# A hybrid DeltaNet and attention block: low parts of the projection weights moved to VectorE, the triangular substitution moved to GpSimd

## The chip, the cores and the metric

The kernel runs on one core of a Trainium2 chip. The metric is the device time of one execution in microseconds, the median of several runs. Engines are named as in the profile: PE is TensorE (PEld its weight loads), DVE is VectorE, ACT is ScalarE, POOL is GpSimd, SP is the engine that issues the transfers.

## The reference, cut to what matters

One layer over 512 latent and 256 context tokens of width 2048. All projections read the same normalised, modulated input `h`. Eight heads run a gated delta rule in chunks of 64 tokens, once in each direction; eight heads run attention with rotary positions; one output projection follows.

```python
qkv_g, z_g, gates, q_a, k_a, v_a, z_a = split_proj(h @ w_in)        # and the same for the context
qkv = silu(centred_conv(qkv_g, conv_w))                             # 5 taps, depthwise
...
# chunk_gated_delta, per head and direction
diff = g_c[..., :, None] - g_c[..., None, :]
decay = where(incl, exp(where(incl, diff, 0.0)), 0.0)
a = where(strict, einsum('nbhid,nbhjd->nbhij', k_beta, k_c) * decay, 0.0)
t_inv = triangular_solve(eye + a, eye, left_side=True, lower=True)  # 64 x 64 per chunk
u = t_inv @ (v_c * b_c)
w = t_inv @ (k_beta * exp(g_c))
def step(s, inp):                                                   # over the chunks, in order
    v_new = u_i - w_i @ s
    o_i = (q_i * exp(g_i)) @ s + intra_i @ v_new
    s = s * exp(g_last) + (k_i * exp(g_last - g_i)).T @ v_new
...
o_gdn = o_lf + flip(o_lb)                                           # the two directions
gdn = rms_norm(o_gdn, gdn_norm_w) * silu(z_g)
y = concatenate([gdn, attention(...) * silu(z_a)]) @ w_out
```

## The kernel before, in words

**Numbers in two parts.** Every large matmul is done in three passes of a fast 32-bit format. A weight piece of 128 x 512 is loaded (`wraw`), ACT casts it to the high part (`whi`), and the difference `wraw - whi` is the low part (`wlo`, line 130, helper `split`). PE multiplies high by high, high by low and low by high. `wraw`, `whi` and `wlo` have three buffers each. The engine that makes the low part is POOL unless the call names another. `proj_steps` makes one projection tile of 128 columns out of four such pieces (line 159); there are 36 of these tiles (k, q, v of the scan heads, k and v of attention, q of attention, and five tiles of attention's gate z), the rest of z is projected later by `z_piece`, and the output weights by the last stage.

**Order of work.** PE's instructions run in program order up to the output projection. For the other engines and for SP's transfers a scheduler lays down each queue's order when the kernel is built, by priority (program order, lowered by a stated offset for `first_of_all`, 2500, and `soon` or the substitution, 1500) and by its own model of the times. On the chip each queue is in order.

**Stages.** (1) Normalisation and the first head's projections, to about 160 us. (2) Eight scans, one head after the other, about 243 to 905 us. (3) Attention with the remaining z projections. (4) Output projection.

**A scan** (`gdn_scan(h)`) has 12 chunk steps, both directions stacked on the partitions. For each step PE multiplies keys and state (`ks`, lines 852 to 857), DVE forms `r` (line 866, two halves), PE applies the triangular inverse `UU` (`ts`, line 875), ACT scales to `vs` and `vn` (879, 882), PE updates (886), and DVE adds the new state `st` (892) to `sd`, the decayed old state, which POOL has made meanwhile (called through `mul`, line 240). Between these, the scan yields three times per step and `pull(n)` puts some `n` columns of projection matmuls for later heads into PE's order (3900, 2700 and 3200 columns). These yields are counted as slots, 35 in a scan.

**Preparing the next head** (`gdn_prep(h + 1)`) is cut into eleven parts which are put in at the slots of `PREP_AT`. In order: transposes of k and their norms (three parts; the third also forms `gr`, the decay, from a broadcast load minus `gcum`, line 681, cut by masks at 684 and raised by ACT); products with decay (the fourth); and in the fifth the matrix `AT`, its transposed blocks `NT`, and the **substitution**: 96 blocks of 16 x 16 (`NE`) are read back through DRAM, and 14 pairs of small operations on `NE` invert them:

```python
for m in range(14, 0, -1):
    n = 15 - m
    ... tv = NE[:, 0:m, m] x NE[:, m, m+1:]      # m x n products per partition
    ... NE[:, 0:m, m+1:] += tv
```

The result goes to DRAM (`nd2`, line 744). Parts six and seven transpose v (`tv`, line 751, two banks of PSUM shared with other small tiles) and scale it into `vtok` on ACT; after the seventh the blocks come back as `DD` (four loads, line 758) and are transposed to `DT` (763). Parts eight to eleven (slots 27 to 33) join the blocks on PE (`pxa` 771, `pxb` 779, `pxy` 801 to 813) into `UU`, with copies by ACT (790), POOL (792) and DVE (821).

During a scan, DVE also does the convolution and SiLU of the heads projected meanwhile (`conv`, lines 217 to 225; `silu`, 237; v's result is `vv`). At a scan's end POOL adds the decayed outputs (`oq`, line 902) before DVE and ACT normalise them. In the last scan there is no next head; `attn_prep` normalises and rotates attention's k and the first q instead (`rope_apply`, product `t2` on POOL, the rest on DVE).

The first head is prepared ahead of the first scan, its parts put in by a list of pulls; two gate steps (`g1`) and head 1's convolutions stand among them.

Of the kernel before, what the change touches and what calls it, by code (L numbers as in the profile page):

```python
# [11 lines left out]
ALU = mybir.AluOpType  # L12
# [56 lines left out]
def build(tc, a):  # L69
    nc = tc.nc  # L70
    V, S, G, T, SY = nc.vector, nc.scalar, nc.gpsimd, nc.tensor, nc.sync
# [31 lines left out]
    def hpass(k, hi, lo):  # L103

        return (hi, [t[:, k] for t in hh]), (hi, [hl(m, k) for m in range(2)]), (lo, [t[:, k] for t in hh])
# [13 lines left out]
    gsc = {}  # L119
# [6 lines left out]
    def split(raw, nm, lo_eng=None):  # L126
        hi = wp.tile([128, 512], F32R, tag="whi", bufs=3, name=f"whi_{nm}")
        lo = wp.tile([128, 512], F32R, tag="wlo", bufs=3, name=f"wlo_{nm}")
        S.copy(hi, raw)  # L129
        (lo_eng or G).tensor_tensor(out=lo, in0=raw, in1=hi, op=ALU.subtract)  # L130
        return hi, lo

    def wpiece(src, nm, shape, lo_eng=None):
        raw = wp.tile([128, 512], F32, tag="wraw", bufs=3, name=f"wraw_{nm}")
        v = raw
        if shape is not None:
            v = raw.rearrange("p (a b) -> p a b", b=shape)
        SY.dma_start(v, src)
        hi, lo = split(raw, nm, lo_eng)
        if shape is not None:  # L140
            hi = hi.rearrange("p (a b) -> p a b", b=shape)
            lo = lo.rearrange("p (a b) -> p a b", b=shape)
        return hi, lo
# [6 lines left out]
    def proj_tile(col, nm, pl, pc=None):  # L150
        for _ in proj_steps(col, nm, pl, pc):
            pass

    def proj_steps(col, nm, pl, pc=None):


        for kq in range(4):
            src = w_in[kq * 512:(kq + 1) * 512, col:col + 128].rearrange("(k p) c -> p k c", p=128)
            hi, lo = wpiece(src, f"{nm}_{kq}", 128)
            passes = [(kq * 4 + k4, n, lw, rt) for k4 in range(4)  # L160
                      for n, (lw, rt) in enumerate(hpass(kq * 4 + k4, hi[:, k4], lo[:, k4]))]

            def one(out, m, k, n, lw, rt):
                T.matmul(out, lhsT=lw, rhs=rt[m], start=k == 0 and n == 0, stop=k == KT - 1 and n == 2,  # L164
                         skip_group_check=True)

            if pc is not None and kq == 0:
                for out, m, n_ in ((pl, 0, SEQ), (pc, 1, CTX)):
                    for x in passes:
                        one(out, m, *x)  # L170
                        yield n_
                continue
            for x in passes:
                one(pl, 0, *x)
                if pc is not None:
                    one(pc, 1, *x)
                yield SEQ if pc is None else SEQ + CTX
# [11 lines left out]
    def btile(shape, nm):  # L189
        return PB.tile(shape, F32, tag="b", name=nm)  # L190
# [45 lines left out]
    def silu(eng, out, x, t):  # L236
        eng.scalar_tensor_tensor(out=out, in0=t, scalar=1.0, in1=x, op0=ALU.add, op1=ALU.mult)

    def mul(eng, out, x, y):
        eng.tensor_tensor(out=out, in0=x, in1=y, op=ALU.mult)  # L240
# [347 lines left out]
    def kq_of(h):  # L588
        if h not in kqs:
            kqs[h] = qkp.tile([128, 8, 128], F32, tag="kq", bufs=3, name=f"kq{h}")  # L590
        return kqs[h]

    def gdn_post_k(h, raw):
        kq = kq_of(h)
        kc = kcs[h] = qkp.tile([128, 2, 2, 64], F32, tag="kc", bufs=2, name=f"kc{h}")
        acc, e, off = conv(8 + h, f"k{h}", raw, True)
        x, y = [t[:, off:off + SEQ].rearrange("p (c t) -> p c t", t=64) for t in (acc, e)]
        silu(V, kq[:, 0:4, 0:64], x[:, 0:4], y[:, 0:4])
        silu(V, kq[:, 4:8, 64:128], x[:, 4:8], y[:, 4:8])
        x, y = [t[:, 0:CTX].rearrange("p (c t) -> p c t", t=64) for t in (acc, e)]  # L600
        silu(V, kc[:, :, 0], x[:, 0:2], y[:, 0:2])
        silu(V, kc[:, :, 1], x[:, 2:4][:, ::-1], y[:, 2:4][:, ::-1])
# [18 lines left out]
    def gdn_prep(h):  # L621


        nm = f"h{h}"
        kq, kc, vv = kqs[h], kcs[h], vvs[h]
        UU, IB = UUs[h % 2], IBs[h % 2]
        col = slice(h * 12, h * 12 + 12)
        gr = gp.tile([128, 12, 64], F32, tag="gr", bufs=1, name=f"gr{nm}")
        for s in range(2):
            src = growd[s:s + 1, col].rearrange("s r t -> s (r t)").to_broadcast([64, 768])  # L630
# [7 lines left out]
        t2 = btile([128, 4, 128], f"t2{nm}")  # L638
# [17 lines left out]
        for p in range(2):  # L656
# [18 lines left out]
                        in0=gsc["beta"][:, col].rearrange("p (v q) -> p v q", v=2),  # L675
                        in1=rk2.unsqueeze(1).to_broadcast([128, 2, 6]), op=ALU.mult)
# [1 line left out]
        mul(V, cc[:, 2], cc[:, 0], gsc["esuf"][:, col])  # L678


        G.tensor_tensor(out=gr, in0=gr, in1=gsc["gcum"][:, col].unsqueeze(2).to_broadcast([128, 12, 64]),
                        op=ALU.subtract)
        for v in range(2):
            V.tensor_tensor(out=gr[:, v * 6:v * 6 + 6], in0=gr[:, v * 6:v * 6 + 6],
                            in1=masks[v].unsqueeze(1).to_broadcast([128, 6, 64]), op=ALU.min)
# [35 lines left out]
        NE = gp.tile([96, 16, 16], F32, tag="NE", bufs=1, name=f"NE{nm}")  # L721
        for half in range(2):
            for blk in range(2):
                b, bi = half * 64 + blk * 32, half * 2 + blk
                cb = slice(blk * 32, blk * 32 + 32)
                for v in range(2):
                    src = AT[b:b + 32, v * 6:v * 6 + 6, cb] if v == half else NT[b:b + 32, :, cb]
# [6 lines left out]
        with tc.high_priority(offset=1500):  # L734
            for m in range(14, 0, -1):
                n = 15 - m
                tv = tm[:, :m * n].rearrange("w (j i) -> w j i", i=n)
                V.tensor_tensor(out=tv, in0=NE[:, 0:m, m:m + 1].to_broadcast([96, m, n]),
                                in1=NE[:, m:m + 1, m + 1:].to_broadcast([96, m, n]), op=ALU.mult)
                V.tensor_tensor(out=NE[:, 0:m, m + 1:], in0=NE[:, 0:m, m + 1:], in1=tv, op=ALU.add)  # L740
        nd2 = nd2s[h % 2]
        for s in range(2):
            ds_ = slice(16 * s, 16 * s + 16)
# [40 lines left out]
        for bi in range(4):  # L784
            half, b = bi // 2, bi * 32
            for v in range(2):
                src = (DD if v == half else DT)[b:b + 32, v * 6:v * 6 + 6]
# [36 lines left out]
    def gdn_scan(h):  # L824

        nm = f"h{h}"
        kq, kc = kqs[h], kcs[h]
# [4 lines left out]
        oq = gp2.tile([128, 2, 4, 128], F32, tag="oq", bufs=1, name=f"oq{nm}")  # L832
        osb = oq[:, 0]
        kss = stile([128, 2, 256], f"ks{nm}", "k")
        steps = [(0, 0), (0, 1), (1, 1), (1, 0)] + [(0, p) for p in range(2, 6)] + [(1, p) for p in range(5, 1, -1)]
        for si, (v, p) in enumerate(steps):
# [8 lines left out]
            if si == 0:  # L845
                r = vtok[:, p]
            else:
                ks = kss[:, si % 2].rearrange("q (d e) -> q d e", d=2)
                r = gp2.tile([128, 128], F32, tag="r", bufs=1, name=f"r{nm}_{si}")
# [9 lines left out]
                with first_of_all():  # L859
# [5 lines left out]
                    for rows, d in halves:  # L865
                        V.scalar_tensor_tensor(out=r[rows], in0=ks[rows, d], scalar=gsc["negeg"][rows, gcol:gcol + 1],  # L866
                                               in1=vtok[rows, p], op0=ALU.mult, op1=ALU.add)
# [31 lines left out]
        ms = gp2.tile([128, 4], F32, tag="ms", bufs=2, name=f"ms{nm}")  # L899
        oc = gp2.tile([128, 8, 64], F32, tag="oc", bufs=1, name=f"oc{nm}")  # L900
        jk = oc[:, 0:2].rearrange("p c t -> p (c t)")
        G.tensor_tensor(out=oq[:, 1], in0=osb, in1=oq[:, 1], op=ALU.add)
        V.tensor_tensor(out=osb, in0=oq[:, 1], in1=o, op=ALU.add)
        for p in range(4):
            S.activation(jk, osb[:, p], AF.Square, accum_out=ms[:, p:p + 1])
# [15 lines left out]
    def swapped(x):  # L921

        return x.rearrange("p t (a s r) -> p (t a) s r", a=2, s=2)[:, :, ::-1]
# [17 lines left out]

    def rope_apply(y, tb, t2):

        mul(G, t2.rearrange("p t (a s r) -> p (t a) s r", a=2, s=2), swapped(y),
            tb[:, 1].rearrange("p t (a s r) -> p (t a) s r", a=2, s=2))
        mul(V, y, y, tb[:, 0])
        V.tensor_tensor(out=y, in0=y, in1=t2, op=ALU.add)
# [76 lines left out]
        split_from(tp.rearrange("p t c -> p (t c)"), *A["qt"])  # L1024

    F1, F2, F3 = 3900, 2700, 3200
    PREP_AT = (0, 2, 4, 6, 8, 10, 12, 27, 29, 31, 33)

    def soon():
        return tc.high_priority(offset=1500)  # L1030
# [4 lines left out]
    with tc.high_priority(offset=4000):  # L1035
        raws = [take(klat, cctx[:, 0]), take(qlat, None), take(vlat, cctx[:, 1], None, V),
                take(klat1, cctx1[:, 0], xraw[0]), take(qlat1, None, xraw[1])]
# [82 lines left out]
    def pull(n):  # L1120
        debt[0] += n
        while debt[0] > 0:
            c = next(feed, None)
            if c is None:
                debt[0] = 0
                return
            debt[0] -= c

    def run(gen, *pulls):

        for n in pulls:
            pull(n)
            if next(gen, gen) is gen:
                return
        for _ in gen:
            pull(2000)

    g0, g1 = gates(0, 1), gates(1, NH)
# [7 lines left out]
    with first_of_all():  # L1146
        next(g0, None)
    prep = gdn_prep(0)
    for i, n in enumerate((3000, 5500, 5500, 4000, 14000, 6000)):
        pull(n)  # L1150
        next(prep, None)
        if i == 4:
            gdn_post_k(1, raws[3])
    pull(3000)
    next(g1)
    pull(9000)
    with first_of_all():
        next(g1)
    gdn_post_q(1, raws[4])
    es_x.close()  # L1160
    run(g1, 14000)
    es1.close()
    gp2 = es_g.enter_context(tc.tile_pool(name="gp2", bufs=1, reuse_waits="tile"))
    UUs.append(gp2.tile([128, 12, 128], F32, name="UU1"))
# [3 lines left out]
    for h in range(NH):  # L1168
# [3 lines left out]
        if h + 1 < NH:  # L1172
            prep, prep_at = gdn_prep(h + 1), PREP_AT
        else:
# [4 lines left out]
            prep, prep_at = attn_prep(), range(1, 36, 2)  # L1179
# [334 lines left out]
    for c in range(4):  # L1514
# [3 lines left out]
        if c < 3:  # L1518
            ops = [PO.tile([128, 512], F32, tag="po", name=f"po{c}_{t}") for t in range(4)]
            for k in range(KT):  # L1520
                hi, lo = wpiece(w_out[k * 128:(k + 1) * 128, cs_], f"wo{c}_{k}", None, V)
# [6 lines left out]
        for k in range(KT):  # L1528
            hi = op_.tile([128, 512], F32R, name=f"wlh{k}")
            lo = op_.tile([128, 512], F32R, name=f"wll{k}")  # L1530
# [5 lines left out]
        for t in range(4):  # L1536
# [5 lines left out]
            f = fr[:, t:t + 1]  # L1542
# [36 lines left out]
```

## Time and profile before

| | |
|---|---|
| median of 3 runs | 1368.79 us (1368.75 to 1371.78) |
| profiled execution | 1373.23 us, of which the span from first to last instruction is 1371.5 |
| mean granted clock of TensorE | 0.979 |
| busy: PE / DVE / ACT / POOL | 1271.3 / 781.6 / 583.7 / 458.2 us |
| the same from 243 to 905 us (the scans) | 611.7 / 382.2 / 309.0 / 270.1 us of 662 |

How to read the rows: a row of a group or of a line gives the source line, the engine, the operation, output and inputs by the program's names, their shapes, and the count. Where three durations stand, they are the shortest, median and longest in ns, followed by when the first and the last one started. A row in order of time begins with the start and the duration in us; "x3" are three instructions in a row, and a bracket gives the engine's idle time before it and what ended that. A row of the list of waits says who waited for whose result: us in total, times, longest. A row by stretch gives the stretch, its length, the busy time and count of each engine, then the clock and the transfers' share and rate.

### The profile page before, as it was taken

To read this page: it belongs to the slowest core of one execution; us is meant where nothing else is said; L and a number is where in the kernel's file an instruction comes from. 1 tells how busy PE (TensorE), PEld (TensorE's weight loads), DVE (VectorE), ACT (ScalarE), POOL (GpSimd) and SP (SyncE) were. 2 spreads that over 40 slices of the span, in tenths; PEclk is the share of its full clock that TensorE was granted. 3 is DMA by queue.
4 is the path that set the end of the run, shared out by engine and by line. 5 is a ranking of instruction groups with operands and counts; after the bars stand their busy time and mean duration, and the time that the engine had idled before them with its cause. 6 is when DMAs were issued, how large, how long until landed. Compare 5 with 4: busy or idle time off the path is not lost. (4 is left out here: it accounts for less than half of the span.)

```text
span 1371.5 us, 24428 instructions
## 1 busy us (share of the span) xinstructions
PE 1271.3 (93%) x9226; PEld 1032.2 (75%) x9226; DVE 781.6 (57%) x1662; ACT 583.7 (43%) x1464; POOL 458.2 (33%) x437
## 2 busy tenths in 40 slices
PE   6899998999899999999899998998999999999997
PEld 4566777877788778877787777777888788777785
DVE  5455594766846666485664524316788877544322
ACT  4222542535345454544545434434455444433211
POOL 1323232434344253434334344443233232020330
PEclk9999999999999999999999999999999999999998
DMA  9999233221332223231222443347344343564212
GB/s 342 323 334 348 56 94 85 60 63 44 71 75 70 50 66 65 71 72 53 51 59 70 98 128 100 89 135 226 108 124 146 100 130 109 189 225 146 92 39 92
DMA packets 227001, 164.54 MB, mean 120 GB/s; under 512 B 62210, under 2 KB 198491, under 8 KB 225859
## 3 DMA queue, kind: packets, MB, share of 16 engines
q1 hardware_dynamic: 226586, 162.87, 40.9%
q8 instruction: 73, 1.20, 0.4%
q14 instruction: 45, 0.37, 0.1%
q10 hardware_dynamic: 297, 0.11, 0.0%
HBM read 148.85 MB, written 14.08 MB: 119 GB/s over the span
## 5 line engine op out<-in xcount | busy, mean ns | idle before, releaser
L130 POOL TENSOR_TENSOR wlo_z<-wraw_z,whi_z 128x512 fp32r<-128x512 f32 x44 | 67.3, 1544 | 141.0 <-ACT whi_z L129 128.3
L240 POOL TENSOR_TENSOR sdh<-sth,egl 128x256 f32<-128x256 f32 x80 | 55.1, 689 | 144.4 <-DVE sth L892 99.7
L866 DVE SCALAR_TENSOR_TENSOR rh<-ksh,negeg,vtokh 64x128 f32<-64x128 f32 x176 | 61.3, 348 | 55.3 <-PE ksh L854 45.5
L871 ACT ACTIVATE oqh<-ksh,egsw 64x128 f32<-64x128 f32 x128 | 46.4, 362 | 103.7 <-DVE rh L866 95.8
L147 PE MATMUL po<-wlo_wo,mh 128*128 128x512 f32 x192 | 77.7, 405 | 3.7 <-DVE wlo_wo L130 3.7
L892 DVE TENSOR_TENSOR sth<-sdh,tsh 128x256 f32<-128x256 f32 x80 | 33.6, 419 | 80.3 <-PE tsh L886 73.1
L148 PE MATMUL po<-whi_wo,ml 128*128 128x512 f32 x192 | 77.6, 404 | 0.0
L146 PE MATMUL po<-whi_wo,mh 128*128 128x512 f32 x192 | 76.9, 403 | 0.5 <-ACT whi_wo L129 0.5
L130 DVE TENSOR_TENSOR wlo_wo<-wraw_wo,whi_wo 128x512 fp32r<-128x512 f32 x48 | 37.7, 793 | 63.8 <-ACT whi_wo L129 63.8
L1360 PE MATMUL zl<-hhL,whi_z 128*128 128x512 f32 x176 | 74.0, 421 | 0.0
L1360 PE MATMUL zl<-hhL,wlo_z 128*128 128x512 f32 x176 | 69.7, 396 | 0.1
L1360 PE MATMUL zl<-hL,whi_z 128*128 128x512 f32 x176 | 69.6, 396 | 0.0
L886 PE MATMUL tsh<-vsh,ktok 128*128 128x128 f32 x352 | 58.2, 289 | 8.7 <-ACT vsh L879 5.6
L886 PEld LDWEIGHTS tsh<-vsh,ktok 128*128 128x128 f32 x352 | 49.1, 197 | 18.8 <-ACT vsh L879 8.7
L1401 DVE SCALAR_TENSOR_TENSOR gacc<-graw,scol,gacc 128x512 f32<-128x512 f32 x60 | 60.0, 1000 | 1.2
L1510 POOL TENSOR_TENSOR yx<-yx,tt 128x512 f32<-128x512 f32 x12 | 17.2, 1445 | 127.9 <-DVE tt L240 127.9
L130 POOL TENSOR_TENSOR wlo_v<-wraw_v,whi_v 128x512 fp32r<-128x512 f32 x28 | 38.1, 1362 | 59.3 <-ACT whi_v L129 59.2
L129 ACT CAST whi_wo<-wraw_wo 128x512 fp32r<-128x512 f32 x48 | 29.3, 618 | 64.9 <-PE po L148 47.9
L875 PE MATMUL tsh<-rh,UU 128*128 128x128 f32 x176 | 36.9, 292 | 18.7 <-DVE rh L866 18.5
L879 ACT ACTIVATE vsh<-tsh,cch 128x128 f32<-128x128 f32 x88 | 32.3, 367 | 46.0 <-PE tsh L875 44.8
L221 DVE SCALAR_TENSOR_TENSOR cacc_v<-craw,cvT,cacc_v 128x512 f32<-128x512 f32 (+1 forms) x64 | 44.1, 734 | 10.5 <-ACT cacc_v L217 10.2
L875 PEld LDWEIGHTS tsh<-rh,UU 128*128 128x128 f32 x176 | 28.7, 190 | 28.3 <-issue 20.4
(542 smaller groups left out, 4147.8 us busy)
## 6 DMA issues: line engine op xcount, KB each, us to landing
wada<-in_w_ada SPq DMA_DIRECT2D x64, 512.0 KB, 8.6
graw<-in_w_ada SPq DMA_DIRECT2D x64, 256.0 KB, 3.3
wraw_wo<-in_w_out SPq DMA_DIRECT2D x48, 256.0 KB, 2.8
wraw_z<-in_w_in SPq DMA_DIRECT2D x44, 256.0 KB, 3.1
wraw_v<-in_w_in SPq DMA_DIRECT2D x28, 256.0 KB, 2.8
wraw_k<-in_w_in SPq DMA_DIRECT2D x24, 256.0 KB, 2.8
wraw_q<-in_w_in SPq DMA_DIRECT2D x24, 256.0 KB, 2.9
xs<-in_x SPq DMA_DIRECT2D x4, 1024.0 KB, 7.4
```

Of the source, the lines that this page charges most:

```text
L130: (lo_eng or G).tensor_tensor(out=lo, in0=raw, in1=hi, op=ALU.subtract)
L146: T.matmul(out, lhsT=lh, rhs=rh, start=start, stop=False, skip_group_check=True)
L147: T.matmul(out, lhsT=lh, rhs=rl, start=False, stop=False, skip_group_check=True)
L148: T.matmul(out, lhsT=ll, rhs=rh, start=False, stop=stop, skip_group_check=True)
L221: V.scalar_tensor_tensor(out=x, in0=raw[:, i0 + j:i0 + j + m], scalar=w(j), in1=x, op0=ALU.mult, op1=ALU.add)
L240: eng.tensor_tensor(out=out, in0=x, in1=y, op=ALU.mult)
L866: V.scalar_tensor_tensor(out=r[rows], in0=ks[rows, d], scalar=gsc["negeg"][rows, gcol:gcol + 1], in1=vtok[rows, p], op0=ALU.mult, op1=ALU.add)
L871: S.activation(oq[rows, v, p - 2], ks[rows, d], AF.Copy, scale=gsc["egsw"][rows, gcol:gcol + 1])
L875: T.matmul(ts[:, 2], lhsT=UU[:, w], rhs=r, start=True, stop=True, skip_group_check=True)
L886: T.matmul(ts[:, d], lhsT=ktok[:, p, half], rhs=vs, start=True, stop=True, skip_group_check=True)
L1360: T.matmul(pl, lhsT=lw, rhs=rt, start=k == 0 and m == 0, stop=k == KT - 1 and m == 2, skip_group_check=True)
L1401: V.scalar_tensor_tensor(out=acc, in0=raw, scalar=scol[:, k:k + 1], in1=acc, op0=ALU.mult, op1=ALU.add)
```

## The change

It moves work between engines and some of it in time:

- `proj_steps` asks for the low parts of its pieces on VectorE (144 pieces). Those of the very first weights and of `z_piece` stay on GpSimd.
- The 28 small operations of each head's substitution go from VectorE to GpSimd (224 in all).
- Three operations go from GpSimd to VectorE: the subtraction in `gr`, the addition in `oq`, and the product in `rope_apply`.
- Parts six and seven of the preparation are put in at slots 15 and 18 instead of 10 and 12.
- In the first head's preparation part six comes later, ahead of the last gate step; the pulls add up to the same columns.

```diff
@@ proj_steps
-            hi, lo = wpiece(src, f"{nm}_{kq}", 128)
+            hi, lo = wpiece(src, f"{nm}_{kq}", 128, V)
@@ gdn_prep
-        G.tensor_tensor(out=gr, in0=gr, in1=gsc["gcum"][:, col].unsqueeze(2).to_broadcast([128, 12, 64]),
+        V.tensor_tensor(out=gr, in0=gr, in1=gsc["gcum"][:, col].unsqueeze(2).to_broadcast([128, 12, 64]),
                         op=ALU.subtract)
@@ gdn_prep, substitution
-                V.tensor_tensor(out=tv, in0=NE[:, 0:m, m:m + 1].to_broadcast([96, m, n]),
+                G.tensor_tensor(out=tv, in0=NE[:, 0:m, m:m + 1].to_broadcast([96, m, n]),
                                 in1=NE[:, m:m + 1, m + 1:].to_broadcast([96, m, n]), op=ALU.mult)
-                V.tensor_tensor(out=NE[:, 0:m, m + 1:], in0=NE[:, 0:m, m + 1:], in1=tv, op=ALU.add)
+                G.tensor_tensor(out=NE[:, 0:m, m + 1:], in0=NE[:, 0:m, m + 1:], in1=tv, op=ALU.add)
@@ gdn_scan
-        G.tensor_tensor(out=oq[:, 1], in0=osb, in1=oq[:, 1], op=ALU.add)
+        V.tensor_tensor(out=oq[:, 1], in0=osb, in1=oq[:, 1], op=ALU.add)
@@ rope_apply
-        mul(G, t2.rearrange("p t (a s r) -> p (t a) s r", a=2, s=2), swapped(y),
+        mul(V, t2.rearrange("p t (a s r) -> p (t a) s r", a=2, s=2), swapped(y),
@@ slots
-    PREP_AT = (0, 2, 4, 6, 8, 10, 12, 27, 29, 31, 33)
+    PREP_AT = (0, 2, 4, 6, 8, 15, 18, 27, 29, 31, 33)
@@ the first head
-    for i, n in enumerate((3000, 5500, 5500, 4000, 14000, 6000)):
+    for n in (3000, 5500, 5500, 4000, 14000):
         pull(n)
         next(prep, None)
-        if i == 4:
-            gdn_post_k(1, raws[3])
-    pull(3000)
+    gdn_post_k(1, raws[3])
+    pull(9000)
     next(g1)
     pull(9000)
     ...
     gdn_post_q(1, raws[4])
     es_x.close()
-    run(g1, 14000)
+    pull(7000)
+    next(prep, None)
+    run(g1, 7000)
```

## The prediction

> **What bounds the kernel now.** I read the page's busy shares first, then the list of what TensorE (PE) waited for, then time-ordered rows around the longest waits.
>
> ```profile
> span 1371.5 us, 24428 instructions
> PE 1271.3 (93%) x9226; PEld 1032.2 (75%) x9226; DVE 781.6 (57%) x1662; ACT 583.7 (43%) x1464; POOL 458.2 (33%) x437
> ```
>
> ```profile
> 243.00:905.00 662.00, 611.65 (x5448) 512.40 (x5449) 382.23 (x944) 309.02 (x876) 270.08 (x264) 0.98 0.29 70
> ```
>
> The last row is the stretch of the eight scans (busy us of PE, PEld, DVE, ACT, POOL): PE is idle there for 662 - 612 = 50 us. PE runs in an order fixed by the program and its work does not change, so only these idle times, and the few before them, can be won. Which they are:
>
> ```profile
> PE tsh L875 <- DVE rh L866: 18.5, 14, 3.4
> PE ksh L852 <- DVE sth L892: 7.0, 10, 1.2
> PE tsh L875 <- DVE UU L821: 6.7, 3, 2.9
> PE tsh L886 <- ACT vsh L879: 5.6, 8, 2.0
> PE tvh L751 <- DVE grh L240: 3.9, 2, 1.9
> PE tsh L886 <- ACT vnh L882: 3.1, 9, 0.8
> PE qtp L955 <- DVE ktok L947: 2.6, 1, 2.6
> ```
>
> ```profile
> PE tvh L751 <- DVE gts__117 L564: 3.8, 1, 3.8
> ```
>
> (us, times, longest; the last from just before the first scan.) Most of it names VectorE (DVE), which is idle 42% of that stretch: it comes late, not too little. Why, around one of the 14 waits:
>
> ```profile
> 282.09 1.29 POOL L130 TENSOR_TENSOR wlo_v<-wraw_v,whi_v 128x512 fp32r<-128x512 f32 x1
> ```
>
> ```profile
> 282.24 1.21 DVE L740 TENSOR_TENSOR NEh<-NEh,tmh 96x56 f32<-96x56 f32 x1
> ...
> 284.35 0.71 DVE L866 SCALAR_TENSOR_TENSOR rh<-ksh,negeg,vtokh 64x128 f32<-64x128 f32 x2
> ```
>
> A substitution step, 0.20 us in the median (its rows stand below), took 1.21 here, the length of the low-part subtraction that GpSimd (POOL) had just begun; rh, on the scan's chain, stood behind it in DVE's queue. [...]
>
> The same at the start of a scan, where UU's last copies wait behind v's conv, and in the attention preparation, where the rope product is on POOL:
>
> ```profile
> 645.54 1.45 POOL L902 TENSOR_TENSOR oqh<-oqh 128x512 f32<-128x512 f32 x1
> 646.95 1.65 POOL L681 TENSOR_TENSOR grh<-grh,gcum 128x768 f32<-128x768 f32 x1
> ```
>
> ```profile
> 647.19 3.16 DVE L237 SCALAR_TENSOR_TENSOR vv<-craw,cacc_v 128x256 f32<-128x256 f32 x3
> 650.37 1.47 DVE L821 COPY UU<-pxyh 32x192 f32<-32x192 f32 x4
> ```
>
> ```profile
> 870.05 1.26 POOL L130 TENSOR_TENSOR wlo_z1a<-wraw_z1a,whi_z1a 128x512 fp32r<-128x512 f32 x1
> ```
>
> ```profile
> 870.13 1.73 DVE L240 TENSOR_TENSOR ktok<-ktok,IB 128x512 f32<-128x512 f32 x1 [1.38 <-POOL rt2k L240]
> 871.79 0.71 DVE L866 SCALAR_TENSOR_TENSOR rh<-ksh,negeg,vtokh 64x128 f32<-64x128 f32 x2
> ```
>
> ```profile
> PE tsh L875 <- DVE rh L866: 5.6, 3, 3.4
> ```
>
> The last row is the wait list from 820 to 905 us alone, the attention preparation. The same list over the substitution of head 1 and of head 7, the first and last of seven, each with one such wait of 1.1 to 1.8 us:
>
> ```profile
> PE tsh L875 <- DVE rh L866: 1.1, 1, 1.1
> ```
>
> ```profile
> PE tsh L875 <- DVE rh L866: 1.8, 1, 1.8
> ```
>
> **The change, part by part.** The rows the prices come from:
>
> ```profile
> L130 DVE TENSOR_TENSOR wlo_wo<-wraw_wo,whi_wo x48: 671/693/1759, 1168.2 to 1310.3; 128x512 fp32r<-128x512 f32 x48
> ...
> L130 POOL TENSOR_TENSOR wlo_q<-wraw_q,whi_q x24: 1267/1292/2064, 255.3 to 671.5; 128x512 fp32r<-128x512 f32 x24
> ```
>
> ```profile
> L383 POOL TENSOR_TENSOR w0l<-w0r,w0h x16: 458/464/1007, 36.2 to 139.3; 128x128 fp32r<-128x128 f32 x16
> ```
>
> ```profile
> 243.00:905.00 662.00, 0.00 (x0) 160.43 (x119) 0.98 0.29 70
> ```
>
> ```profile
> 243.00:905.00 662.00, 58.12 (x203) 0.98 0.29 70
> ```
>
> (The rows by stretch are line 130 alone, DVE then POOL; the last is the tile NE on DVE.) No matmul, ACT instruction or transfer is added or removed.
>
> *Low parts.* There are 36 projection tiles of four pieces, 144; 119 of them lie in the scan stretch, where POOL loses 160 us and DVE gains 119 x 0.69 = 82 us (144 x 0.69 = 99 in all). No PE wait names a low part of the scans, so the faster piece wins nothing itself. What it wins is that POOL no longer holds DVE for 1.3 us at a time.
>
> *Substitution.* Off DVE go 58 us in the scan stretch. On POOL a step has on average 40 elements per partition (m(15-m), m = 1 to 14). The two POOL subtractions, 0.458 us for 128 elements and 1.267 for 512, give 2.1 ns per element and 0.19 us fixed, so 0.27 us; with some 0.05 between dependent steps and 0.13 for meetings with DVE, both estimates, 28 x 0.45 = 12.6 us a head. PE does not notice until the substitution outlasts its room, read from the shortest and the longest of seven scan heads:
>
> ```profile
> L740 DVE TENSOR_TENSOR NEh<-NEh,tmh x14: 170/203/1269, 694.1 to 704.1; 96x14 f32<-96x14 f32 x2, 96x26 f32<-96x26 f32 x2, 96x36 f32<-96x36 f32 x2, 96x44 f32<-96x44 f32 x2
> L763 DVE STREAM_TRANSPOSE DTh<-DDh x1: 579/579/579, 710.5 to 710.5; 128x384 f32<-128x384 f32 x1
> L771 PE MATMUL pxah<-DTh,grh x48: 191/191/212, 718.5 to 719.3; 32*32 32x32 f32 x48
> ```
>
> ```profile
> L740 DVE TENSOR_TENSOR NEh<-NEh,tmh x14: 168/199/1217, 602.8 to 611.3; 96x14 f32<-96x14 f32 x2, 96x26 f32<-96x26 f32 x2, 96x36 f32<-96x36 f32 x2, 96x44 f32<-96x44 f32 x2
> L771 PE MATMUL pxah<-DTh,grh x48: 191/191/212, 630.6 to 631.5; 32*32 32x32 f32 x48
> ```
>
> From the last step (704.3) to the transposed DD (711.1) the two DRAM trips cost 6.8 us. The first step to pxa is 24 us in the short head, 28 in the long one, so the substitution may last 17 to 21 us, 19 on average; now it lasts about 10. At 12.6 it stays hidden: 0 taken, 1 us kept for a head or two. [...]
>
> Gains: rh's waits outside the attention preparation are 18.5 - 5.6 = 12.9 us, sth's 7.0. Seven of rh's, about 1.5 us each, and five of sth's, about 1 us each, stand beside substitution steps: some 15 us; the rest stands beside conv. All 19.9 is one bound, zero the other; I take 10, since conv and the new low parts remain in front of rh.
>
> *v's transposes from slots 10 and 12 to 15 and 18.* The 3.9 us waits were for the PSUM bank that DVE frees late after gr's products; some five slots later it is free: -3.9 (0 to -3.9). With them move vtok's six ACT copies and, past SP's other loads, the four DD loads and DT's transpose. All are emitted after slot 18 but before 27, and need the substitution anyway: 0. In head 0 the order changes the same way (the first transposes of v 6000 columns and a gate step later); the 3.8 us wait there is for a copy (gts) that queued behind substitution steps: -3 (0 to -3.8).
>
> *gr's subtraction, oq's addition, rope's product to DVE.* Each adds DVE time (8 x about 1.0, 8 x 0.69, 3 x 0.69). The price of the first two is 0.69 for 512 elements by the row of wlo_wo and in proportion for 768. At a scan's start the three vv operations took 3.16 us beside POOL; four of them without it:
>
> ```profile
> 185.53 1.17 DVE L237 SCALAR_TENSOR_TENSOR vv<-craw,cacc_v 128x256 f32<-128x256 f32 x4
> ```
>
> So they would take about 0.9, while 0.69 + 1.0 come on DVE: of 6.7 us I take -4 (+1 to -5.8). In the attention preparation a POOL product of 1.27 and a blocked 1.73 become two times 0.69: of 5.6 + 2.6 I take -4 (0 to -7).
>
> *Price of the low parts on DVE.* DVE's queue is in order, so a low part that waits for ACT's high part holds rh and sth behind it, and PE behind them. No row shows it. Lower bound: the work left on DVE, 382 - 58 = 324 us, beside which 19.9 - 15 = 5 us of PE waits stand, 0.015 per us, so 99 x 0.015 = 1.5 us. Upper: the substitution's own rate, about 15 us of waits per 58 us, so 26 us. A low part is one long operation like a conv tap rather than 28 chained ones; I take 7.
>
> *Queues.* On POOL, sd (the scan state's decay) now stands behind small steps instead of 1.3 us pieces, and the steps behind an sd that waits for sth. SP's store of the substitution waits with it, as it does now; loads behind it have up to 10.7 us:
>
> ```profile
> SPq L744 <- DVE NEh L740: 20.4, 7, 4.1
> SPq L138 <- POOL wlo_k L130: 109.5, 23, 10.7
> ```
>
> SP already waits that long for low parts and no PE wait names a weight load: 0.
>
> **Sum.** -10 - 3.9 - 3 - 4 - 4 + 7 + 1 = -17 us. The profiled execution took 1373.2 us (span 1371.5 and 1.7 around it), so 1356; the median of the three runs, 1368.8, is 4.4 lower, so 1352 is forecast.
>
> **Rivals.** [...]
> *Low parts block the chain (no change).* At the upper 26 us instead of 7, the gains, 24.9 less 1, are eaten: about +2 to -3, 1366 to 1371. For it: POOL now idles long for the same high parts, 54 us for those of v alone. Against it: DVE is idle for 280 us of the stretch.
>
> ```profile
> POOL wlo_v L130 <- ACT whi_v L129: 53.6, 21, 7.8
> ```
>
> *More is won.* All waits named go, at the lower price: -19.9 - 3.9 - 3.8 - 5.8 - 7 + 1.5 = -38.9, 1330; I count from 1330 to 1343.
> *The waits only move.* vs on ACT, already 5.6 us, is late next, and half is won: about -8, 1361. The scan's chain is short, but ACT is at 47% there.
>
> **How the numbers follow.** Chances: forecast (1343 to 1358) 40%, more won 14%, waits move (1358 to 1364) 16%, no change 14%, slower 16%. A change under 0.3%, 4 us, can't be told from none. So faster 70%, same 13%, slower 17%. The range 1338 to 1377 leaves out some 7% below and 11% above; the forecast's own is 1343 to 1358.
>
> **What would show it.** Right: NE's steps on POOL at 0.25 to 0.45 us, a head's substitution under 17 us, no PE wait for pxa's DT; the three vv operations at a scan's start near 1 us instead of 3.16; the waits for rh down to 8 us or less, for grh and gts gone. Wrong: substitution of 20 us or more, PE waiting for DT or UU, SP waiting longer for NE than for low parts; or new PE waits for rh with DVE idle on a high part of ACT.

## The result, and the profile after

The changed kernel takes 1331.8 us in the median, against 1370.1 for the kernel before on the same chip: a ratio of 0.972 (95% interval 0.970 to 0.974), 38 us. The forecast was 1352, its range 1338 to 1377: the direction was right, but the gain was more than twice as large as forecast and the time lies below the range.

The page after, the lines that answer to the first two shown of before:

```profile
span 1328.1 us, 24396 instructions
PE 1257.2 (95%) x9226; PEld 1022.5 (77%) x9226; DVE 794.5 (60%) x1601; ACT 584.4 (44%) x1464; POOL 313.8 (24%) x498
```

TensorE has the same 9226 instructions. Its idle time falls from 1371.5 - 1271.3 = 100.2 us to 70.9, by 29; its busy time falls too, by 14 us. This second part was in no term of the sum. (The two profiled executions differ by 43 us, more than the medians' 38: the one before lies above its median, the one after is the shortest of its four.) The list of what TensorE waited for, whole span:

```profile
PE ksh L852 <- DVE sth L892: 8.8, 7, 2.1
...
PE tsh L886 <- ACT vsh L879: 3.0, 5, 0.8
...
PE qtp L955 <- DVE ktok L947: 2.8, 1, 2.8
PE tsh L886 <- ACT vnh L882: 2.4, 4, 0.8
PE kvl L164 <- DVE wlo_kv L130: 2.1, 1, 2.1
...
PE tsh L875 <- DVE UU L821: 1.8, 3, 0.9
...
PE tsh L875 <- DVE rh L866: 0.9, 2, 0.6
```

The waits for rh are nearly gone (18.5 before), those for grh and gts are gone (7.7), UU's are down from 6.7 to 1.8. The one for ktok stays, sth's have grown from 7.0 to 8.8, and one for a low part (wlo_kv) is new. On VectorE the long operations are gone: the taps of v's convolution, before and after (shortest, median, longest in ns):

```profile
L221 DVE SCALAR_TENSOR_TENSOR cacc_v<-craw,cvT,cacc_v x64: 468/742/1699, 179.7 to 719.2; 128x512 f32<-128x512 f32 x32, 128x256 f32<-128x256 f32 x32
```

```profile
L221 DVE SCALAR_TENSOR_TENSOR cacc_v<-craw,cvT,cacc_v x64: 469/742/875, 177.3 to 688.6; 128x512 f32<-128x512 f32 x32, 128x256 f32<-128x256 f32 x32
```

Of all 160 taps of the convolutions (median 0.74 us), 15 took over 1 us before (1.03 to 1.78), each beside an operation of GpSimd that was running meanwhile, 11 times a low part; after the change none did.

**The part that no wait shows.** Rows by stretch, whose third figure from the end is the granted clock. Both pairs hold the same wait of 2.0 us in the attention stage (for qTl), first before, then after:

```profile
985.40:988.80 3.40, 1.36 (x8) 0.89 (x7) 3.30 (x6) 1.25 (x3) 1.46 (x1) 1.00 0.91 289
988.80:992.20 3.40, 3.40 (x13) 3.11 (x14) 1.74 (x4) 0.59 (x1) 0.00 (x0) 0.50 0.32 94
```

```profile
940.90:944.30 3.40, 1.71 (x10) 1.19 (x8) 3.26 (x6) 1.60 (x3) 1.45 (x1) 1.00 0.90 287
944.30:947.70 3.40, 3.06 (x21) 2.74 (x22) 2.33 (x6) 0.59 (x1) 0.00 (x0) 1.00 0.40 114
```

In these traces the clock changes on a grid of 3.41 us: within each, the starts of the half-clock stretches lie whole multiples of 3.413 us apart, to 0.01 us. After a window in which TensorE was busy for 1.36 us, the next one ran at 0.50; after one with 1.71 us it stayed at 1.00. The same was read for every window at full clock from 150 us on, in all fourteen traces: whenever TensorE was busy for less than 43% of a window, the next ran at half clock; above 58% none did; between, both occur. So an idle time of 2 us within one window was always followed by a window at half clock, in which up to 1.7 us are lost (an estimate, half of the 3.41; experiment 7 measured 1.55), and the same wait cut by a window's edge could cost nothing more, as in the second pair. The mean granted clock is 0.979 before and 0.988 after, from which an estimate is 1371.5 x 0.021 = 29 us lost before and 1328.1 x 0.012 = 16 after. Between 150 us and the last multiplications there are twelve half-clock windows before and five after. These 13 us are nearly all of the 14 by which the same instructions were busy for less.

### The profile page after: what moved, and what is told of

It reads as the page before. It is cut to its first block, busy times and chain, and to the rows that moved or that the text cites. A ratio compares the mean times of both kernels' runs of the same rounds, so it can differ in the third digit from the quotient of the medians.

```text
span 1328.1 us, 24396 instructions
## 1 busy us (share of the span) xinstructions
PE 1257.2 (95%) x9226; PEld 1022.5 (77%) x9226; DVE 794.5 (60%) x1601; ACT 584.4 (44%) x1464; POOL 313.8 (24%) x498
## 5 line engine op out<-in xcount | busy, mean ns | idle before, releaser
L866 DVE SCALAR_TENSOR_TENSOR rh<-ksh,negeg,vtokh 64x128 f32<-64x128 f32 x176 | 61.2, 348 | 33.8 <-PE ksh L854 27.1
L886 PEld LDWEIGHTS tsh<-vsh,ktok 128*128 128x128 f32 x352 | 47.4, 190 | 13.9 <-ACT vnh L882 5.7
L147 PEld LDWEIGHTS po<-wlo_wo,mh 128*128 128x128 f32 x192 | 36.6, 190 | 15.3 <-DVE wlo_wo L130 6.8
L950 ACT CAST pth<-pt 128x512 fp32r<-128x512 f32 x48 | 26.9, 585 | 47.7 <-PE pt L1289 47.7
L164 PE MATMUL vl<-hhL,wlo_v 128*128 128x512 f32 x112 | 46.3, 413 | 0.0
L164 PE MATMUL vl<-hhL,whi_v 128*128 128x512 f32 x112 | 46.2, 412 | 0.0
```

The source lines that it names most:

```text
L147: T.matmul(out, lhsT=lh, rhs=rl, start=False, stop=False, skip_group_check=True)
L886: T.matmul(ts[:, d], lhsT=ktok[:, p, half], rhs=vs, start=True, stop=True, skip_group_check=True)
```

## The experiments

Theory A is that GpSimd's 1.3-us low parts, which block VectorE (beside one a tap of 0.74 us in the median took up to 1.78), carry the gain. Theory B is that the substitution's 28 steps in VectorE's queue do.

**1. One part alone.** Edits to the kernel before: the low parts on VectorE (`wpiece(..., 128, V)` and nothing else), or the substitution on GpSimd (`G` for `V` in its two lines and nothing else).

> Before, with only the low parts of the projection pieces on VectorE. [...] If the substitution's 28 steps in VectorE's queue are the cause by themselves (theory B), the added 99 us on VectorE bring 0 to +8 us.

Measured: 1340.7 us, ratio 0.977 (0.974 to 0.980). Its waits:

```profile
PE tvh L751 <- DVE grh L240: 5.9, 2, 3.0
...
PE kvl L164 <- DVE wlo_kv L130: 4.7, 1, 4.7
PE tsh L875 <- DVE UU L821: 3.7, 3, 1.4
PE tsh L875 <- DVE rh L866: 3.3, 7, 1.0
```

The gain of 31 us is on theory A's side, and theory B's loss (0 to +8 us) did not come. rh falls from 18.5 to 3.3 with the substitution still on VectorE, and the wait for gts is gone with the first head's order unchanged. The substitution's steps themselves lose their long cases (longest 1274 ns before, 611 here). Two of the 160 taps still take over 1 us, both beside gr's subtraction, which is on GpSimd here.

> Before, with only the substitution on GpSimd. Theory A: VectorE's convolutions still meet GpSimd's 1.3 us pieces, and the steps queue behind them, a head's substitution takes over 16 us; gain 5 to 15 us. Theory B: the waits for rh and sth beside the substitution (15 us) vanish and dips with them, gain 20 us or more.

Measured: 1375.6 us, ratio 1.003 (1.001 to 1.005): slower by 3 us, where both theories had a gain. The waits stay, and 20 of the taps take over 1 us:

```profile
PE tsh L875 <- DVE rh L866: 17.6, 10, 3.4
PE ksh L852 <- DVE sth L892: 7.4, 9, 1.5
```

VectorE now waits for what GpSimd does: 37.0 us in all with DT's transpose at the head of its queue (the transfer of DD comes behind the substitution), 27.1 us for sd.

**2. One part undone.** Edits to the changed kernel: the low parts back on GpSimd, or the substitution back on VectorE.

> The changed kernel, with the low parts back on GpSimd. Theory A: about as e_sub with the slots and small moves added, 1343 to 1355. Theory B: within 5 us of the changed kernel, 1332 to 1337.

Measured: 1359.3 us, ratio to before 0.990 (0.988 to 0.991): 27 of the 38 us are lost. That is above theory A's range, and far from theory B's. rh's waits are back, and 21 of the taps take over 1 us:

```profile
PE tsh L875 <- DVE rh L866: 12.3, 12, 4.3
PE ksh L852 <- DVE sth L892: 7.1, 8, 2.5
```

> The changed kernel, with the substitution back on VectorE. Theory A: most of the gain stays, 1334 to 1345, with the steps at 0.20 us on VectorE. Theory B: it is lost, 1355 or more.

Measured: 1328.2 us, ratio 0.967 (0.965 to 0.969). It is faster than the changed kernel, and below theory A's range. No tap takes over 1 us. So theory A carries nearly all, theory B falls, and the substitution's move cost about 3.5 us in either setting by the medians (6.7 here by the ratios to before). Where, the rows in order of time of VectorE show, near the end of the last substitution; first the changed kernel, then this one:

```profile
754.12 0.58 DVE L763 STREAM_TRANSPOSE DTh<-DDh 128x384 f32<-128x384 f32 x1 [4.50 <-DMA DDh<-nd]
754.63 0.65 DVE L130 TENSOR_TENSOR wlo_q5a<-wraw_q5a,whi_q5a 128x512 fp32r<-128x512 f32 x1
755.31 0.42 DVE L892 TENSOR_TENSOR sth<-sdh,tsh 128x256 f32<-128x256 f32 x1
```

```profile
748.74 0.69 DVE L130 TENSOR_TENSOR wlo_q5a<-wraw_q5a,whi_q5a 128x512 fp32r<-128x512 f32 x1 [2.23 <-ACT whi_q5a L129]
749.46 0.42 DVE L892 TENSOR_TENSOR sth<-sdh,tsh 128x256 f32<-128x256 f32 x1
...
751.81 0.58 DVE L763 STREAM_TRANSPOSE DTh<-DDh 128x384 f32<-128x384 f32 x1
```

With the steps on GpSimd, DT's transpose stands at the head of VectorE's queue waiting for DD for up to 4.5 us (23.2 in all; nothing in this run), and the addition of the new state behind it; TensorE waits 2.1 us there, and half clock follows (0.50 from 756.6 to 760.0). Six of the seven waits for sth in the changed kernel (7.8 of 8.8 us) stand behind such a transpose. The seventh, 1.0 us at 444, is the other queue: sd stands behind all 28 steps on GpSimd. SP's queue shows the delay too, its store of the substitution waiting 60.2 us in all where it was 21.4 before:

```profile
SPq L744 <- POOL NEh L740: 60.2, 8, 11.3
```

Matching the two traces' matmuls, the changed kernel is 6.3 us behind at the end of the scans, 3.6 of it from 755 and the rest from 290, 450, 530 and 600, each beside a wait for sth. After the scans 3.6 us come back, where half-clock windows fall differently in the two runs.

**3. DT's transpose later** (the changed kernel, `yield` ahead of `V.transpose(out=flat3(DT), ...)`, a slot 24 put into `PREP_AT`).

> The changed kernel with the transpose of the substituted DD into DT put some slots later (its own part of the preparation, at slot 24, in place of the end of the part at slot 18). In the changed kernel it stands in VectorE's in-order queue waiting up to 8.0 us for the transfer behind GpSimd's substitution, and copies of the state (sth) queue behind it: waits of 1.98, 1.87 and 2.09 us at 288, 599 and 754, the last with a half-clock stretch of 1.7 us. Theory B2 (this is why the substitution on GpSimd costs 3.6 us against the same kernel with it on VectorE, 1331.8 against 1328.2): the three waits go, 1325 to 1328. [...] Rival H (the transfers behind it, of DT to the other partitions, now come late for UU): UU's waits grow from 1.8 to over 6 us and the time is over 1334.

Measured: 1336.7 us, ratio 0.975 (0.972 to 0.977): a miss. The scheduler put the transpose into VectorE's queue at the same place, ahead of the same sth, so the edit did not do what it says, and theory B2 stays untested: that DT's transpose costs the 3.5 us is read from rows, and no run shows it. Rival H's time came without its sign, since UU's waits are 1.6 us. The two rows show the wait of VectorE still there (23.2 us in the changed kernel) and TensorE's for sth at 11.6:

```profile
DVE DTh L764 <- DMA DDh<-nd: 25.8, 8, 4.8
```

```profile
PE ksh L853 <- DVE sth L893: 11.6, 8, 2.2
```

**4. The two small parts alone.** Edits to the kernel before: the slots of v's transposes and the first head's order; or the three small operations (gr, oq, rope) on VectorE.

> The kernel before with the later slots of the v transposes (15 and 18 in place of 10 and 12, and the first head's order) alone. Theory A (each part's gain is its waits): the waits of the transposes for gts and grh (7.7 us) go, the half-clock stretches after those at 217.4 and 681.6 too (3.4 us), while rh and UU stay as they are (18.5 and 6.7 us): 1361 to 1365. [...]

Measured: 1364.7 us, ratio 0.994 (0.992 to 0.996), as theory A had it in time, though not in place: grh's wait is gone, the one for gts is not.

```profile
PE tsh L875 <- DVE rh L866: 16.3, 14, 3.4
...
PE tvh L751 <- DVE gts__117 L564: 3.8, 1, 3.8
```

> The kernel before with three small operations on VectorE in place of GpSimd (the subtraction from gr, the sum in oq, the first product of the rope), the low parts left on GpSimd. [...] Rival F (the first product of the rope lies on the chain of the attention's preparation, as the prediction put it, worth 4 us, and gr's on that of the substitution): 1362 to 1366.

Measured: 1361.3 us, ratio 0.992 (0.990 to 0.994): a little under rival F's range. The waits of the attention preparation alone (812 to 895 us) show rh at 2.2 us where it was 5.6, and ktok unmoved; UU's, over the whole span, are not less but 6.9. So of rival F the rope's product is borne out, gr's part is not; and of the 8 us between this profile and the one before, some 5 are half clock (nine windows where there were twelve):

```profile
PE qtp L955 <- DVE ktok L947: 2.5, 1, 2.5
PE tsh L875 <- DVE rh L866: 2.2, 2, 1.3
```

The four parts alone sum to -31.4 + 3.4 - 7.7 - 11.0 = -47 us, against -38 together. Some waits were won twice: rh's in the attention preparation (5.6 us) fall to 1.0 by the low parts alone and to 2.2 by the three small operations alone, and gts' goes with the low parts although the slots were meant for it.

**5. Is it GpSimd's occupation, or the low parts' being late themselves?** The changed kernel, with the same subtraction made once more on GpSimd, where no matmul waits for it:

```diff
+        if lo_eng is V and nm[:2] != "wo":
+            G.tensor_tensor(out=raw, in0=raw, in1=hi, op=ALU.subtract)
```

> The changed kernel, with the low parts of the scans' pieces on VectorE as they are there, and the same subtraction made a second time on GpSimd, into the piece's raw tile, which no engine reads afterwards (it holds that tile for its next load about as long as in the kernel before). So GpSimd works as much as in the version with the low parts put back on it (1359.3 us), and no matrix multiplication waits for what it does. Theory A (GpSimd's 128x512 subtractions slow VectorE's two-operand work while they run, and that is where the low parts' gain comes from): VectorE's conv operations have maxima of 1.7 us again, the waits for rh come back (12 us), and the time is 1352 to 1364. Rival I (the low parts gained because they are no longer themselves late for the matrix multiplications and no longer queue with sdh and the substitution): 1331 to 1337.

Measured: 1383.2 us, ratio to before 1.009 (1.006 to 1.011), 51 us over the changed kernel. That is beyond theory A's range, and rival I is excluded. Both of VectorE's troubles are back:

```profile
PE ksh L854 <- DVE sth L894: 19.6, 13, 3.1
PE tsh L877 <- DVE rh L868: 10.3, 15, 1.7
```

```profile
L223 DVE SCALAR_TENSOR_TENSOR cacc_q<-craw,cvT,cacc_q x28: 740/752/1789, 170.5 to 700.3; 128x512 f32<-128x512 f32 x28
```

Long taps (12 of the 160 over 1 us, none in the changed kernel) and rh's waits are the blocking. The larger part here, sth's, goes with VectorE waiting for sd, which queues on GpSimd behind the extra work: 13.9 us, where it was 3.7 in the changed kernel. The extra operation also holds the raw tile longer than in the changed kernel, but the only wait of TensorE for a piece of the scans' weights grows by no more than 2.2 us (wlo_kv, 2.1 to 4.3). So the run shows that GpSimd's occupation alone takes back the gain, not how its 51 us divide.

**6. What the low parts cost on VectorE.** The kernel before, with the scans' low parts made nowhere and the high part used in their place; this leaves a part of the computation out.

> The kernel before without the 144 low parts of the scans' pieces: no engine makes them, and TensorE takes the high part in their place (the output is not the reference's; its matrix multiplications, their number and their shapes are the same). With them made on VectorE this kernel took 1340.7 us, with them on GpSimd 1372, so this one splits those 31 us into what GpSimd's release wins and what the 99 us of subtractions on VectorE cost. The prediction's term (they cost 7 us, by holding rh and sth in VectorE's queue): 1331 to 1336. The lower bound of that term (1.5 us, VectorE has room): 1337 to 1341. If the release of GpSimd is not what wins, but the low parts being ready earlier, their absence gains about as much again over VectorE's version: under 1331, and the waits for rh stay above 8 us.

Measured: 1325.8 us, ratio 0.966 (0.964 to 0.969). GpSimd's release is worth 3.4% or 46 us (before, no wait of TensorE names a low part of the scans, so their readiness adds little), and making the parts on VectorE costs 1.1% or 15 of them. The time lies below the two ranges that were put down for the prediction's term; it lies in the third, under 1331, but that one's other sign (rh's waits above 8 us) did not come. The 15 us are not paid where the prediction looked. rh's waits are the same with the parts on VectorE (3.3) and without them (3.8); what goes is the wait for wlo_kv (4.7) and half of grh's (5.9 to 3.1). Matching the two traces' matmuls, 9 of the 12 us between them lie ahead of the first scan, between 160 and 206 us, where the wait for wlo_kv and three windows of half clock stand with the parts on VectorE and none without:

```profile
PE tsh L878 <- DVE rh L869: 3.8, 6, 1.0
...
PE tsh L878 <- DVE UU L824: 3.5, 3, 1.8
PE tvh L754 <- DVE grh L243: 3.1, 2, 2.0
```

**7. Does half clock cost time, or is it only recorded?** The kernel before, with dummy multiplications of the unit matrix ahead of waits after which the clock fell, six places in the first run, three of them in the second:

```diff
+    def keep_warm(out, n):
+        for _ in range(n):
+            T.matmul(out, lhsT=ident, rhs=ident, start=True, stop=True, skip_group_check=True)
...
+            keep_warm(ts[:, 0], {(1, 0): 11, (5, 0): 11, (7, 3): 7, (7, 7): 13}.get((h, si), 0))
```

> The kernel before, with 58 extra TensorE multiplications of the unit matrix (128x128, some 0.22 us each by their four passes), whose results are overwritten: they stand in front of six waits after which the granted clock fell to 0.5 for 3.4 us (those of 2.0 to 3.4 us at 323.1 and 648.3 for UU, 744.4 for vsh, 839.7 and 869.3 for rh, 893.4 for ktok), and last as long as these or a little less. The computation is unchanged, and so is every wait of the other engines. Theory C (the 12 us of the gain that the waits do not account for are such stretches of half clock, each of which costs 1.7 us): the six stretches go, the waits are filled, and the time falls by 6 x 1.7 = 10 us, less up to 3 us where a row of dummies outlasts its wait: 1361 to 1366, granted clock 0.979 to 0.985. Rival D (the clock is only recorded so, or falls for another reason than the idle time of TensorE): no stretch goes, and the time is 1371 to 1375, slower by what the dummies outlast.

Measured: 1375.5 us, ratio 1.003 (1.001 to 1.004), slower, with a better clock (0.985, as theory C had it) but rival D's time. The eleven dummies at 321.6 took 2.62 us, 0.24 each: about four times the 0.058 of 128 columns in the fast format (an estimate from the 0.23 us between the starts of two matmuls of 512 columns), which is all that the trace shows of four passes. The scheduler counts the dummies and changed ScalarE's order: beside the first of them vs now stands behind och's and oq's work. A new wait of 3.7 us follows, with two windows of half clock behind it:

```profile
PE tsh L892 <- ACT vsh L884: 8.4, 8, 3.7
```

> The kernel before with the extra multiplications of the unit matrix only at three places: 7 and 13 in front of the waits for rh at 839.7 and 869.3, 9 in front of the one for ktok at 893.4, where the earlier run with six places kept the order of ScalarE, VectorE and TensorE as it was and won 1.5 to 1.7 us each, while at two of its other places the written order of ScalarE changed and a wait of 3.7 us for vsh stood up. Theory C (a stretch of half clock costs its 1.7 us, and filled waits win it back): the three stretches at 842.0, 872.8 and 896.7 go, TensorE's work from 837 to 900 takes some 5 us less, and the time falls by 5 us, to 1366 to 1368, ratio 0.996. Rival D (what is won there is lost later): ratio 0.999 to 1.002.

Measured: 1367.9 us, ratio 0.998 (0.996 to 0.9997): a gain of about 2.6 us, between the two ranges. In place, theory C holds: half clock costs time. Matmuls from the first of the places, before and then filled:

```profile
841.68 0.46 PE L875 MATMUL tsh<-rh,UU 128*128 128x128 f32 x2 [1.98 <-DVE rh L866]
841.89 0.64 PE L164 MATMUL qal7a<-hhL,whi_q7a 128*128 128x512 f32 x1
...
845.53 0.48 PE L164 MATMUL qal7a<-hhL,wlo_q7a 128*128 128x512 f32 x1
```

```profile
841.91 0.49 PE L880 MATMUL tsh<-rh,UU 128*128 128x128 f32 x2
842.16 0.48 PE L164 MATMUL qal7a<-hhL,whi_q7a 128*128 128x512 f32 x1
...
844.21 0.48 PE L164 MATMUL qal7a<-hhL,wlo_q7a 128*128 128x512 f32 x1
```

From the tsh matmul to the same later matmul it is 3.85 us at half clock and 2.30 filled: 1.55 us won. From 843 to 900, with all three places, 4.4 us are won. But the filled run's profile has half clock at 457, 611 and 778, which this profile of before had not, behind waits of the same length (1.6 to 1.9 us): the grid falls differently on these waits in the two runs, and the total depends on how many waits are near half a window.

**8. A version that beats both.** The substitution back on VectorE, nine dummies ahead of the wait for ktok, and in the attention stage the product with z's half (1.7 us on VectorE) moved behind the split of the next head's q:

```diff
-        if u < NZA:
-            ... silu(V, M[8 + u], M[8 + u], e)
         fill(FQ)
         if more:
             ...
                 qt = attn_qt(h + 1, qn)
+        if u < NZA:
+            ... silu(V, M[8 + u], M[8 + u], e)
```

> The changed kernel with the substitution back on VectorE (1328.2 us), with 9 multiplications of the unit matrix ahead of the wait for ktok at 844.7 (as a filled wait), and in the attention stage the gate's product with the half-made z (1.7 us on VectorE) put behind the split of the next head's q instead of ahead of it: the transposes of the probabilities wait there for that split, 3.3 and 2.0 us at 906 and 938, each with a half-clock stretch behind. If VectorE's order is what these waits are for, they fall to 1.6 and 0.3 us and both stretches go: with the filled wait at 847, -2 x 1.7 -2 x 1.7 -1.6 = 8 us, 1320 to 1323. If the split only finds another operation ahead of it (VectorE is busy four fifths of that stage), the waits stay and only the filled wait counts: 1326 to 1328.

Measured: 1323.0 us, ratio 0.966 (0.963 to 0.968), against the changed kernel's 0.972. Against the version of experiment 2 with the substitution on VectorE (0.967, 0.965 to 0.969) the intervals overlap, so the two further edits are not shown to gain in total. In place they do about what was expected: the waits for qTl fall from 8.1 to 5.3 us, and the half clock behind the two at 906 and 938, and behind the one for ktok, is gone:

```profile
PE pt L1295 <- DVE qTl L955: 5.3, 4, 2.4
```

## Why the prediction was right or wrong

The mechanism it put first, GpSimd's low parts blocking VectorE in front of rh, was right and is shown by experiments 1, 2 and 5: the taps over 1 us and rh's waits all but vanish whenever the low parts leave GpSimd, and come back when that work is put on it again. The sum failed by two of its terms, the clock and the price; two more came out right only in part or by errors that cancel.

- **The clock, put at nothing: "PE runs in an order fixed by the program and its work does not change, so only these idle times ... can be won".** This is the step that failed most. The order stayed, but the time of the same matmuls fell by 14 us, 13 of them by the clock. The row by stretch quoted there showed 0.98 for the scans, and the reading stopped at the idle time. Of the 22 us by which the gain was larger than forecast, this is the largest part. Experiment 7 shows that a half-clock window costs time, 1.55 us in one place.
- **The price of the low parts on VectorE, +7.** In the changed kernel the one wait that shows it is 2.1 us (wlo_kv). Alone the price is 15 us, inside the bounds of 1.5 and 26, but the mechanism named, rh and sth held behind a low part, isn't there (experiment 6): most is paid ahead of the first scan, where TensorE waits for a low part itself. "No PE wait names a low part of the scans" held before the change and not after it.
- **rh and sth, -10 of a bound of 19.9, and the substitution, +1.** Outside the attention preparation rh fell from 12.9 to 0.4 and sth rose from 7.0 to 8.8: 10.7 together, as forecast, but by two errors that cancel. With the substitution undone (experiment 2) the two are 1.9 and 0.2, so the low parts' move wins nearly the whole bound: "conv and the new low parts remain in front of rh" was the argument for half, and they do remain, but at 0.7 us they end in time. And the substitution's move cost nearly all of sth's 8.8 us, where the prediction had 1 for it and 0 for the queues.
- **How the substitution costs.** The steps took 0.28 us in the median, against the 0.27 worked out, and a head 9.8 to 13.2 us against 12.6; no row taken before shows the 0.05 and 0.13 us added to each step, but their sum came out. UU's waits did not grow, and the slower kernel, to which 16% were given, did not come near. What was left at 0 are the queues: "All ... need the substitution anyway: 0" did not ask what stands behind DT's transpose on VectorE, and sd behind the steps was priced at nothing. The rows of experiment 2 show both; that they are the 3.5 us is not tested by a run, since experiment 3 did not move the transpose.

```profile
L740 POOL TENSOR_TENSOR NEh<-NEh,tmh x112: 208/284/731, 203.6 to 747.7; 96x14 f32<-96x14 f32 x16, 96x26 f32<-96x26 f32 x16, 96x36 f32<-96x36 f32 x16, 96x44 f32<-96x44 f32 x16
```

Right in size: v's transposes (-3.9: the wait is gone, experiment 4). gts' -3 came (-3.8), but by the release of GpSimd and not by the first head's order, which alone left it at 3.8. UU's -4 came (-4.9) in the whole, but the three small operations that it was put down to do not bring it alone (6.9). Of the attention preparation's -4, 5.0 came in rh and nothing in ktok; the low parts alone take rh there from 5.6 to 1.0. The rival in which vs is late next did not come: its waits fell from 5.6 to 3.0.

"More is won" forecast 1330, within 2 us. It did so by a sum of 38.9 us of idle time; what came was 29 us of idle time and 13 of clock, so its number is largely luck, though its argument, that the waits go together once the blocking goes, was the better one for rh.

## What to carry to other kernels

When one engine's long operations block another's, price their removal by all the waits behind the blocked engine, and look at the granted clock beside the idle time: in this kernel a TensorE wait of about 2 us (1.98) cost 1.55 us again in the window after it. Moving chained work to an idle engine can lose if its result then comes late to a queue of the busy one: ask what stands behind the first instruction that consumes it. A change in several parts is tested by each part alone and each undone; here one of the four was a loss that the other three hid.

## What the runs showed of the hardware that was not expected

- In the fourteen traces half clock followed every window of 3.41 us in which TensorE was busy for less than 43%, and none in which it was busy for more than 58%. The place of the grid differs between traces: the half-clock windows start 2.37 us past a multiple of 3.413 us, counted from the first instruction, in the trace of before, and 2.24 us in the one after. One such window cost 1.55 us where it could be measured with the same matmuls on both sides.
- GpSimd's small chained steps (14 to 56 elements on 96 partitions) took 0.28 us in the median where VectorE takes 0.20. That is a ratio of 1.4, less than the 1.9 for 128x512 (1.29 against 0.69 us). Their long cases are blocking in the other direction: in the changed kernel 28 of the 224 steps took over 0.6 us, and each overlapped a tap or a low part of VectorE that took 0.68 to 0.84 us.
